# A hybrid decoder layer on one core: four layer-norm products and 24 weight low halves change engine

## The chip, the cores and the metric

The kernel runs on one NeuronCore of a Trainium2 chip. The metric is device time in microseconds (us), the median of the runs. TensorE (PE in the profile, PEld its weight loads) multiplies matrices, VectorE (DVE), ScalarE (ACT) and GpSimd (POOL) work element by element, SyncE (SP) issues most DMAs. Each engine takes its own instructions strictly in the order of its queue.

## The reference, cut to what matters

One decoder layer over 512 tokens of width 1024. RMS-normed input `h` is projected once, and three token mixers use the columns:

```python
proj = h @ w_in[i]
nq, nkv, ngate, nz, su, sv, sz, rs, rz, mg = _split_cols(proj)
y_nsa = _nsa(q, kc, vc, ks, vs, kw, vw, gate, ...)          # attention
y_sg  = _spatial_gating(su, sv, ln_g, ln_b, w_s, b_s)       # spatial gating
y_rk  = _rwkv7(rs, ...)                                     # chunked recurrence
ys = stack([y_nsa * silu(nz), y_sg * silu(sz), y_rk * silu(rz)])
...
# in _spatial_gating:
vn = ((vf - mu) * lax.rsqrt(var + LN_EPS)) * ln_g + ln_b
mixed = einsum('gts,bcsgd->bctgd', tril(w_s), vn) + b_s.T
return u * mixed
```

Then come a gated merge of the three branches, an output projection, a gated per-layer embedding and a last RMS norm.

## The kernel before, in words

**Products in two halves.** Every large product is computed with operands split into a rounded high half (type fp32r) and the rest, a low half, as three matmuls per slice of 128 rows: high x high, high x low, low x high. `wload` (L69 to L79) brings one piece of weights: SP issues a DMA into `wr` (a ring of 4 buffers, L75), ScalarE rounds it into `wh` (5 buffers, L77), and the engine that stands in `ph_["l"]` subtracts it to make `wl` (5 buffers, L78). `ph_["l"]` is a switch that the kernel sets as it goes along; `wload` reads it when it is called. A piece has at most 560 columns in all, so a block of 128 columns takes two pieces (four slices each) and a chunk of 256 or 280 columns takes four pieces (two slices each).

`fm_block` gives the product with channels on partitions: 24 matmuls of 512 columns in one PSUM tile, then an evacuation. `tm_chunk` gives it with tokens on partitions: four PSUM tiles (t = 0 to 3), 24 matmuls each, and an evacuation behind each. Both take their PSUM tile from the same two buffers (`mm_ps`), so the third tile waits until the first has been evacuated.

**The order around the change.** The recurrence runs over 8 chunks `c`, each a chain that goes from TensorE to ScalarE and VectorE and back (`r_ps`, `u_ps`, `st_ps`, copies L544 to L565; at every second chunk the norm of the output with a power on GpSimd, L587, and VectorE's L588). Projections fill TensorE meanwhile, in this order: `su`, `sv`, six merge gates `sg`, the gate `sz` of the spatial gating (L619 to L630), then `rz` and `nz` (L680 to L690). Between them stands the spatial gating itself: the layer norm of `sv`, which comes back from DRAM (L652), with statistics on VectorE (L654), the power on GpSimd (L658), and for each of 4 row tiles a subtract and multiply on VectorE (L660), the multiplication with `ln_g` on GpSimd (L661) and the addition of `ln_b` on VectorE (L662). The `sz` evacuation is a tanh on ScalarE (L624) and a product on VectorE (L625); that of `rz` and `nz` is L684 and L685.

Then the recurrence and the `sz` to `nz` buffers are closed, y1 and `rz` come back from DRAM (L713, L718), are multiplied (L719, VectorE) and split (L705 ScalarE, L706 VectorE). The attention's projections follow: values and gates in one `tm_chunk` of 280 columns (evacuation L734 to L737, ScalarE and VectorE in turn), four `fm_block`s of queries (L742 to L747), two of keys (L754 to L757). Attention and the merges come after.

The text fixes the dependencies; the order of each engine's queue is made by the tile framework's planner (`schedule_with_timeline_sim=True`), which lists the instructions by its own simulated times and gives those that stand earlier in the text precedence. `tc.issue_after` pins a few of them. In the kernel before, `ph_["l"]` is GpSimd in all of the pieces for `sz`, `rz`, `nz`, and of the attention's projections.

Of the kernel before, what the change touches and what calls it, by code (L numbers as in the profile page):

```python
# [13 lines left out]
OP = mybir.AluOpType  # L14
# [25 lines left out]
def f(ap):  # L40
    return ap.bitcast(F32)
# [3 lines left out]
def hybrid_kernel(ctx, tc, x, p, norm_g, w_in, cmp_w1, cmp_w2, cmp_pe, sg_ln_g, sg_ln_b, sg_w, sg_b,  # L45
# [3 lines left out]
    V, S, G, PE, SY = nc.vector, nc.scalar, nc.gpsimd, nc.tensor, nc.sync  # L49
# [10 lines left out]
    def mm(o, a, b, start, stop, **kw):  # L60
        return PE.matmul(o, a, b, start=start, stop=stop, **kw).ins  # L61


    ph_ = {"l": V}
# [16 lines left out]
    def wparts(segs, nk):  # L81
        per = WE // sum(s[2] for s in segs)
        hs, ls = [], []
        for k0 in range(0, nk, per):
            kn = min(per, nk - k0)
            h, l = wload([(w, c0, cn, k0) for w, c0, cn in segs], kn)
            for k in range(kn):
                hs.append(h[:, k, :])
                ls.append(l[:, k, :])
        return hs, ls  # L90
# [58 lines left out]
    def fm_block(c0, n, evac, w=None, srcH=None, srcL=None, nk=8, pool=None):  # L149
        hs, ls = wparts([(w_in if w is None else w, c0, n)], nk)  # L150
        sH, sL = (hH, hL) if srcH is None else (srcH, srcL)
        ps = pmm.tile([128, 512], F32, tag="mm", name="mm_ps")
        for k in range(nk):
            mm(ps[:n], hs[k], sH[:, k, :], k == 0, False)
            mm(ps[:n], hs[k], sL[:, k, :], False, False)
            mm(ps[:n], ls[k], sH[:, k, :], False, k == nk - 1)
        evac(ps)

    def tm_chunk(segs, srcH, srcL, nk, evac):
        n = sum(s[2] for s in segs)  # L160
        hs, ls = wparts(segs, nk)
        for t in range(4):
            ts = slice(t * 128, (t + 1) * 128)
            ps = pmm.tile([128, 512], F32, tag="mm", name="mm_ps")
            for k in range(nk):
                mm(ps[:, :n], srcH[:, k, ts], hs[k], k == 0, False)
                mm(ps[:, :n], srcH[:, k, ts], ls[k], False, False)
                mm(ps[:, :n], srcL[:, k, ts], hs[k], False, k == nk - 1)
            evac(t, ps)
# [359 lines left out]
    for c in range(8):  # L529
# [41 lines left out]
        if u == 1:  # L571
            t = c // 2
# [23 lines left out]
    for nm, off in (("su", O_SU), ("sv", O_SV)):  # L596
        for hf in range(2):
            ph_["l"] = V if (nm, hf) in LV else G
            def ev_t(t, ps, nm=nm, hf=hf):
                st = stp.tile([128, 512], F32, tag="st", name="st")  # L600
                if nm == "sz":
                    S.activation(st[:, 0:256], ps[:, 0:256], AF.Tanh, scale=0.5)
                    V.scalar_tensor_tensor(st[:, 0:256], st[:, 0:256], 1.0, ps[:, 0:256], op0=OP.add, op1=OP.mult)
                else:
                    S.copy(st[:, 0:256], ps[:, 0:256])
                SY.dma_start(dr[nm][t * 128:(t + 1) * 128, hf * 256:hf * 256 + 256], st[:, 0:256])
            tm_chunk([(w_in, off + 256 * hf, 256)], hH, hL, 8, ev_t)
    for m in range(NG):
# [5 lines left out]
        with ExitStack() as es:  # L614
            if ("sg", m) in CH:
                es.enter_context(tc.issue_after(canch[CH["sg", m]]))
            fm_block(O_MG + 1024 + m * 128, 128, ev_m)

    for nm, off in (("sz", O_SZ),):  # L619
        for hf in range(2):  # L620
            def ev_t(t, ps, nm=nm, hf=hf):
                st = stp.tile([128, 512], F32, tag="st", name="st")
                if nm == "sz":
                    S.activation(st[:, 0:256], ps[:, 0:256], AF.Tanh, scale=0.5)  # L624
                    V.scalar_tensor_tensor(st[:, 0:256], st[:, 0:256], 1.0, ps[:, 0:256], op0=OP.add, op1=OP.mult)  # L625
                else:
                    S.copy(st[:, 0:256], ps[:, 0:256])
                SY.dma_start(dr[nm][t * 128:(t + 1) * 128, hf * 256:hf * 256 + 256], st[:, 0:256])
            tm_chunk([(w_in, off + 256 * hf, 256)], hH, hL, 8, ev_t)
    sg_ctx = ExitStack()  # L630
    sp = sg_ctx.enter_context(tc.tile_pool(name="sp", bufs=2))

    z0 = sp.tile([128, 512], F32, tag="z", name="z0", bufs=1)
    lng = sp.tile([128, 512], F32, tag="lng", name="lng", bufs=1)
# [12 lines left out]
    vn = sp.tile([128, 4, 512], F32, tag="vn", name="vn", bufs=1)  # L647
# [10 lines left out]
    G.tensor_tensor(rs4, rs4, mhalf[:, 0:4], OP.pow)  # L658
    for t in range(4):
        V.tensor_scalar(vn[:, t, :], vn[:, t, :], mv[:, t, 0:1], rs4[:, t:t + 1], op0=OP.subtract, op1=OP.mult)  # L660
        G.tensor_tensor(vn[:, t, :], vn[:, t, :], lng, OP.mult)  # L661
        V.tensor_tensor(vn[:, t, :], vn[:, t, :], lnb, OP.add)  # L662
    for g in range(8):
        ps = rps.tile([128, 4, 64], F32, tag="s", name="mx_ps")
# [64 lines left out]
    vst = nsa.tile([128, 4, 2, 2, 128], R, name="vst")  # L729
    gate = nsa.tile([128, 4, 24], F32, name="gate")  # L730

    def ev_v(t, ps):
        pv = ps[:, 0:256].rearrange("p (b g d) -> p b g d", b=2, g=2)
        S.copy(vst[:, t, :, :, 0:64], pv)  # L734
        V.tensor_tensor(vst[:, t, :, :, 64:128], pv, f(vst[:, t, :, :, 0:64]), OP.subtract)
        S.activation(gate[:, t, :], ps[:, 256:280], AF.Tanh, scale=0.5)  # L736
        V.tensor_scalar(gate[:, t, :], gate[:, t, :], 0.5, 0.5, op0=OP.mult, op1=OP.add)  # L737
    tm_chunk([(w_in, O_NVS, 128), (w_in, O_NVW, 152)], hH, hL, 8, ev_v)

    for q in range(4):  # L740
# [8 lines left out]
    for b in range(2):  # L749
# [7 lines left out]
                V.tensor_tensor(K[o, g, 1, :], ps[a], f(K[a, g, 0, :]), OP.subtract)  # L757
        fm_block((O_NKS, O_NKW)[b], 128, ev_k)


    gp = ctx.enter_context(tc.tile_pool(name="gp", bufs=2))
    macc = gp.tile([128, 8, 512], F32, name="macc", bufs=1)
# [223 lines left out]
```

## Time and profile before

| | us |
|---|---|
| median of 3 runs | 767.99 (767.72, 767.99, 1015.65) |
| the profiled execution, device time | 766.05 |
| its span | 764.3 |
| TensorE busy | 729.1 (95%) |
| VectorE busy | 398.3 (52%) |
| ScalarE busy | 353.8 (46%) |
| GpSimd busy | 325.7 (43%) |

The span is the stretch from the first to the last instruction that the profiler saw; the 1.75 us to the device time lie around it. Busy shares are means over the span; what a change is worth in one stretch is read from the instructions in that stretch and from what TensorE waits for there.

### The profile page before, as it was taken

Reading aid. Unit: us, or ns where it says so; the run is one execution under the profiler, and the core shown is the slowest. Engines: PE = TensorE matmul, PEld = TensorE weight load, DVE = VectorE, ACT = ScalarE, POOL = GpSimd, SP = SyncE. Lnnn points to the kernel's source line nnn. Section 1 sums busy time; section 2 is a strip of 40 time slices with the busy share of each in tenths; the row PEclk is TensorE's granted clock in tenths of the full one; section 3 lists DMA queues with packets and bytes.
Section 4 is the critical chain, followed back from the end, with each engine's and each line's share of the span. In section 5 each row is a group of like instructions: output and inputs, shape, how many; then the busy total and the mean of one; then the engine's idle time right before and its main releaser. Section 6 shows DMA issues by size and latency. Waiting matters only on the chain.

```text
span 764.3 us, 13017 instructions
## 1 busy us (share of the span) xinstructions
PE 729.1 (95%) x4910; PEld 617.9 (81%) x4910; DVE 398.3 (52%) x748; ACT 353.8 (46%) x744; POOL 325.7 (43%) x304
## 2 busy tenths in 40 slices
PE   4899999999999899999899999989999999999996
PEld 4888877899877888778777777867877888998995
DVE  6531387758826642444649455477664222226335
ACT  6455455543362333333456564466654333226453
POOL 6444541120245443423644334534344666255563
PEclk9999999999999999999999999999999999999999
DMA  6843222125535453444533222311116433222222
GB/s 200 189 112 89 56 69 62 36 90 153 147 107 196 112 148 89 115 153 146 155 86 110 70 56 56 82 29 42 42 42 218 141 96 106 88 92 75 84 69 110
DMA packets 106688, 78.71 MB, mean 103 GB/s; under 512 B 5569, under 2 KB 97282, under 8 KB 106626
## 3 DMA queue, kind: packets, MB, share of 16 engines
q1 hardware_dynamic: 105890, 75.27, 34.5%
q10 hardware_dynamic: 736, 2.63, 0.8%
q8 instruction: 38, 0.62, 0.3%
q14 instruction: 24, 0.20, 0.1%
HBM read 67.91 MB, written 9.96 MB: 102 GB/s over the span
## 4 chain that ended last, share of the span: by engine, by line
PE 82%; DVE 7%; DMA 4%; ACT 3%; issue 2%; POOL 1%; SPq 1%; ACTq 0%; POOLq 0%; DVEq 0%
PE mm_ps L61 64%; PE s_ps L61 3%; PE o_ps L61 2%; PE g_ps L61 2%; PE p_ps L850 2%; PE Yp L61 1%; PE hid L61 1%; DMA vn<-dr_sv 1%; DMA xs__129<-in_x_dram 1%; DMA zs<-dr_nz 1%; DVE vn L662 1%; DVE mx L836 1%; ACT wh L77 1%; DVE vn L660 1%; PE mx_ps L61 1%
## 5 line engine op out<-in xcount | busy, mean ns | idle before, releaser
L78 POOL TENSOR_TENSOR wl<-wr,wh 128x512 fp32r<-128x512 f32 (+1 forms) x168 | 224.5, 1344 | 306.4 <-ACT wh L77 288.1
L77 ACT CAST wh<-wr 128x512 fp32r<-128x512 f32 (+1 forms) x194 | 119.3, 620 | 173.9 <-PE mm_ps L61 114.2
L61 PE MATMUL mm_ps<-hH,wh 128*128 128x512 f32 (+1 forms) x440 | 174.4, 396 | 6.4 <-ACT gate L736 2.7
L61 PE MATMUL mm_ps<-hH,wl 128*128 128x512 f32 (+1 forms) x440 | 172.7, 393 | 0.4 <-DVE wl L78 0.4
L61 PE MATMUL mm_ps<-hL,wh 128*128 128x512 f32 (+1 forms) x440 | 172.7, 393 | 0.0
L61 PEld LDWEIGHTS mm_ps<-hH,wh 128*128 128x128 f32 x440 | 83.6, 190 | 25.0 <-ACT gate L736 3.4
L61 PEld LDWEIGHTS mm_ps<-hH,wl 128*128 128x128 f32 x440 | 83.4, 190 | 18.6 <-DVE wl L78 0.6
L61 PEld LDWEIGHTS mm_ps<-hL,wh 128*128 128x128 f32 x440 | 83.4, 190 | 16.9 <-issue 0.4
L61 PE MATMUL mm_ps<-wh,hH 128*128 128x256 f32 (+1 forms) x224 | 64.2, 288 | 4.5 <-DVE st L625 3.3
L61 PE MATMUL mm_ps<-wh,hL 128*128 128x256 f32 (+1 forms) x224 | 64.0, 287 | 0.0
L61 PE MATMUL mm_ps<-wl,hH 128*128 128x256 f32 (+1 forms) x224 | 63.7, 285 | 0.0
L61 PEld LDWEIGHTS mm_ps<-wh,hH 128*128 128x128 f32 x224 | 42.0, 188 | 6.4 <-DVE st L625 3.5
L61 PEld LDWEIGHTS mm_ps<-wl,hH 128*128 128x128 f32 x224 | 42.1, 188 | 0.6
L61 PEld LDWEIGHTS mm_ps<-wh,hL 128*128 128x128 f32 x224 | 42.1, 188 | 0.6 <-issue 0.2
L854 DVE TENSOR_TENSOR pl<-p_ps,ph 128x512 fp32r<-128x512 f32 x40 | 27.1, 684 | 26.8 <-ACT ph L853 26.6
L61 PE MATMUL mm_ps<-ysH,wh 128*128 128x512 f32 x96 | 38.6, 402 | 0.3 <-ACT ysH L705 0.3
L61 PE MATMUL mm_ps<-ysL,wh 128*128 128x512 f32 x96 | 38.4, 400 | 0.2 <-DVE ysL L706 0.2
L61 PE MATMUL mm_ps<-ysH,wl 128*128 128x512 f32 x96 | 38.2, 398 | 0.0
L837 ACT ACTIVATE P<-s_ps,mx 128x512 f32<-128x512 f32 (+3 forms) x64 | 33.4, 531 | 7.9 <-DVE mx L836 5.5
L61 PE MATMUL mm_ps<-wh,mH 128*128 128x256 f32 x128 | 36.2, 287 | 0.6 <-DVE x L899 0.6
L61 PE MATMUL mm_ps<-wl,hT 128*128 128x256 f32 x128 | 35.8, 281 | 0.0
L61 PE MATMUL mm_ps<-wh,hT 128*128 128x256 f32 x128 | 35.8, 285 | 0.0
(336 smaller groups left out, 1450.4 us busy)
## 6 DMA issues: line engine op xcount, KB each, us to landing
wr<-in_w_in_dram SPq DMA_DIRECT2D x130, 256.0 KB
wr<-in_w_branch_dram SPq DMA_DIRECT2D x24, 256.0 KB
wr<-in_w_o_dram SPq DMA_DIRECT2D x16, 256.0 KB
wr<-in_w_ple_gate_dram SPq DMA_DIRECT2D x16, 256.0 KB
xs__129<-in_x_dram SPq DMA_DIRECT2D x4, 512.0 KB
w1t<-in_cmp_w_dram SPq DMA_DIRECT2D x4, 512.0 KB
x<-in_x_dram ACTq DMA_DIRECT2D x4, 512.0 KB
out_dram<-x SPq DMA_DIRECT2D x8, 256.0 KB
```

What stands on the lines that cost most here:

```text
L61: return PE.matmul(o, a, b, start=start, stop=stop, **kw).ins
L77: S.copy(h[:, :m], raw[:, :m])
L78: ph_["l"].tensor_tensor(l[:, :m], raw[:, :m], f(h[:, :m]), OP.subtract)
L660: V.tensor_scalar(vn[:, t, :], vn[:, t, :], mv[:, t, 0:1], rs4[:, t:t + 1], op0=OP.subtract, op1=OP.mult)
L662: V.tensor_tensor(vn[:, t, :], vn[:, t, :], lnb, OP.add)
L836: V.tensor_reduce(mx[:, hh:hh + 1], s_ps[:, :W], axis=AX.X, op=OP.max, negate=True)
L837: S.activation(P[:, hh, :W], s_ps[:, :W], AF.Exp, bias=mx[:, hh:hh + 1], accum_out=sm[:, hh:hh + 1])
L850: PE.transpose(p_ps[:, hh * 128:hh * 128 + 128], P[:, hh, kt * 128:kt * 128 + 128], ident)
L854: V.tensor_tensor(pl, p_ps, f(ph), OP.subtract)
```

## The change

Three edits. The low halves of the 8 pieces for `sz` go from GpSimd to VectorE; the multiplication with `ln_g` (4 instructions, L661) goes from GpSimd to VectorE; the low halves of the 16 pieces for the attention's projections (4 for values and gates, 8 for queries, 4 for keys) go from GpSimd to VectorE. `rz`, `nz` and everything behind the keys stay as they are. No DMA, no matmul and no buffer changes.

```diff
@@ -616,6 +616,7 @@
             fm_block(O_MG + 1024 + m * 128, 128, ev_m)
 
+    ph_["l"] = V
     for nm, off in (("sz", O_SZ),):
         for hf in range(2):
             def ev_t(t, ps, nm=nm, hf=hf):
@@ -627,6 +628,7 @@
             tm_chunk([(w_in, off + 256 * hf, 256)], hH, hL, 8, ev_t)
+    ph_["l"] = G
     sg_ctx = ExitStack()
@@ -658,7 +660,7 @@
     for t in range(4):
         V.tensor_scalar(vn[:, t, :], vn[:, t, :], mv[:, t, 0:1], rs4[:, t:t + 1], op0=OP.subtract, op1=OP.mult)
-        G.tensor_tensor(vn[:, t, :], vn[:, t, :], lng, OP.mult)
+        V.tensor_tensor(vn[:, t, :], vn[:, t, :], lng, OP.mult)
         V.tensor_tensor(vn[:, t, :], vn[:, t, :], lnb, OP.add)
@@ -728,6 +730,8 @@
     gate = nsa.tile([128, 4, 24], F32, name="gate")
+
+    ph_["l"] = V
 
     def ev_v(t, ps):
@@ -757,6 +761,7 @@
         fm_block((O_NKS, O_NKW)[b], 128, ev_k)
 
+    ph_["l"] = G
 
     gp = ctx.enter_context(tc.tile_pool(name="gp", bufs=2))
```

## Rows read from the trace of the kernel before

**Rows 1.** The page: busy us, share of the span, instructions of each engine.

```profile
PE 729.1 (95%) x4910; PEld 617.9 (81%) x4910; DVE 398.3 (52%) x748; ACT 353.8 (46%) x744; POOL 325.7 (43%) x304
```

**Rows 2.** Stretches: length, busy us of PE, PEld, DVE, ACT, POOL, clock, DMA.

```profile
225.00:254.00 29.00, 24.75 (x247) 20.98 (x247) 17.52 (x29) 6.09 (x14) 13.69 (x10) 1.00 0.59 180
254.00:350.00 96.00, 95.94 (x868) 80.74 (x867) 40.75 (x92) 33.01 (x64) 38.21 (x28) 1.00 0.41 120
350.00:372.00 22.00, 18.08 (x111) 15.84 (x110) 15.84 (x24) 10.80 (x24) 8.68 (x6) 1.00 0.56 168
372.00:402.00 30.00, 30.00 (x137) 24.14 (x136) 12.73 (x20) 14.56 (x25) 13.88 (x11) 1.00 0.41 118
```

**Rows 3.** TensorE in order of time: start, length, instruction, [idle before, releaser].

```profile
243.02 0.28 PE L61 MATMUL mm_ps<-wl,hH 128*128 128x256 f32 x1
...
250.77 0.39 PE L61 MATMUL mm_ps<-wh,hH 128*128 128x256 f32 x1 [3.34 <-DVE st L625]
...
357.88 0.40 PE L61 MATMUL mm_ps<-wh,hH 128*128 128x280 f32 x1 [1.19 <-ACT gate L736]
...
369.78 0.50 PE L61 MATMUL mm_ps<-hH,wh 128*128 128x512 f32 x1 [2.06 <-ACT gate L736]
```

**Rows 4.** VectorE in order of time, 233 to 251 and 347 to 350 us.

```profile
233.12 0.69 DVE L654 BATCH_NORM_STATS2 bs<-vn 128x6 f32<-128x512 f32 x1 [9.67 <-DMA vn<-dr_sv]
...
239.92 4.80 DVE L660 TENSOR_SCALAR vn<-vn,mv,rs 128x512 f32<-128x512 f32 x4 [0.48 <-POOL rs L658]
244.64 5.74 DVE L662 TENSOR_TENSOR vn<-vn,lnb 128x512 f32<-128x512 f32 x4
250.31 0.41 DVE L625 SCALAR_TENSOR_TENSOR st<-st,mm_ps 128x256 f32<-128x256 f32 x1
...
347.86 1.77 DVE L588 TENSOR_TENSOR yc<-yc,va 128x512 f32<-128x512 f32 x1 [3.55 <-POOL va L587]
349.54 0.68 DVE L685 SCALAR_TENSOR_TENSOR st<-st,mm_ps 128x512 f32<-128x512 f32 x1
```

**Rows 5.** Single lines: count, duration ns min/median/max, first and last start.

```profile
L660 DVE TENSOR_SCALAR vn<-vn,mv,rs x4: 534/1495/1510, 239.9 to 243.2; 128x512 f32<-128x512 f32 x4
L662 DVE TENSOR_TENSOR vn<-vn,lnb x4: 678/1756/1775, 244.6 to 249.7; 128x512 f32<-128x512 f32 x4
L588 DVE TENSOR_TENSOR yc<-yc,va x4: 691/1754/1766, 260.1 to 347.9; 128x512 f32<-128x512 f32 x4
L719 DVE SCALAR_TENSOR_TENSOR vt<-vt,par,zs x4: 739/1774/1780, 361.4 to 366.7; 128x512 f32<-128x512 f32 x4
L78 POOL TENSOR_TENSOR wl<-wr,wh x168: 1272/1302/2449, 21.1 to 747.2; 128x512 fp32r<-128x512 f32 x164, 128x560 fp32r<-128x560 f32 x4
L78 DVE TENSOR_TENSOR wl<-wr,wh x26: 675/691/1552, 16.7 to 199.0; 128x512 fp32r<-128x512 f32 x26
```

**Rows 6.** GpSimd in order of time, 241 to 248 and 344 to 368 us.

```profile
241.49 6.07 POOL L661 TENSOR_TENSOR vn<-vn,lng 128x512 f32<-128x512 f32 x4 [0.36 <-DVE vn L660]
247.53 1.71 POOL L78 TENSOR_TENSOR wl<-wr,wh 128x512 fp32r<-128x512 f32 x1
...
344.82 1.40 POOL L78 TENSOR_TENSOR wl<-wr,wh 128x560 fp32r<-128x560 f32 x1 [6.97 <-ACT wh L77]
346.18 1.64 POOL L587 TENSOR_TENSOR va<-va,mhalf 128x8 f32<-128x8 f32 x1
...
361.38 6.54 POOL L78 TENSOR_TENSOR wl<-wr,wh 128x512 fp32r<-128x512 f32 x4 [12.30 <-ACT wh L77]
```

**Rows 7.** ScalarE in order of time, 239 to 244 and 347 to 358 us.

```profile
239.58 0.62 ACT L77 CAST wh<-wr 128x512 fp32r<-128x512 f32 x1
...
243.85 0.38 ACT L624 ACTIVATE st<-mm_ps 128x256 f32<-128x256 f32 x1 [2.60 <-PE mm_ps L61]
...
347.39 0.59 ACT L684 ACTIVATE st<-mm_ps 128x512 f32<-128x512 f32 x1
...
357.12 0.63 ACT L705 ACTIVATE ysH<-zs 128x512 fp32r<-128x512 f32 x1 [3.09 <-DMA zs<-dr_y]
```

**Rows 8.** The chain that ended last, in order of time: start, length, what.

```profile
350.25 4.20 DMA dr_nz<-st
...
355.87 3.94 DMA zs<-dr_y
```

## The prediction

> **What bounds the kernel now.** I read four views in this order. The page's busy times come first: TensorE is busy for 729.1 of 764.3 us, no other engine for more than 52% [rows 1]. So an edit on VectorE or GpSimd can pay only where TensorE stands still, and the most it could ever return is the 35.2 us left. The busy times by stretch show where that is around the change [rows 2]: from 225 to 254 us TensorE idles 4.25 us, from 254 to 350 only 0.06, from 350 to 372 it idles 3.92, from 372 to 402 nothing. The change works in exactly these four stretches, so 4.25 + 3.92 = 8.2 us is the ceiling of what it can give directly.
>
> TensorE's own timeline says what those waits are [rows 3]. One of 3.34 us ends at 250.77 with VectorE's L625, the evacuation of the first `sz` tile: the third tile needs its PSUM buffer. Two of those between 350 and 372 are 1.19 us (to 357.88) and 2.06 us (to 369.78), both released by L736, the gate of the value chunk on ScalarE; the remaining 0.67 of the 3.92 are small.
>
> VectorE's and GpSimd's timelines give the cause of the first. ScalarE's tanh for that tile starts at 243.85 and takes 0.38 [rows 7]; L625 could run at 244.2, and runs at 250.31, because VectorE is filled without a gap from 239.92 by the four L660 and the four L662 [rows 4]: 10.46 us. Those eight are slow there: 1.5 and 1.76 us at the median against 0.534 and 0.678 for the quickest of the same shape [rows 5], and all the while GpSimd runs L661 and then a low half [rows 6]. A VectorE instruction beside a GpSimd one in this stretch takes some 1 us longer; the same pair of prices stands at L588 and L719 [rows 5].
>
> **The change part by part.** The switch is read when `wload` is called, so the edit moves what it names: 8 + 16 low halves and 4 products. GpSimd loses 4 x 1.5 (from L661's 6.07) + 24 x 1.30 = 37 us; VectorE gains 4 x 0.678 + 24 x 0.69 = 19.3 us [rows 5, 6]. Neither sum lies on the path as a whole. No instruction is added and no DMA is issued elsewhere.
>
> *Layer norm with the `sz` low halves.* Without GpSimd beside it, the block from 239.92 is 4 x 0.534 + 8 x 0.678 = 7.56 us. One low half falls inside it: its high half is made at 239.58 [rows 7], and GpSimd made it behind the L661 at 247.53 [rows 6]; 0.69 more, 8.25. Against 10.46 the block ends 2.2 us earlier, and so does L625. If the planner sets L625 in at 244.2, the whole 3.34 goes; if all of the contention stayed, nothing would be won: ends 0 and 3.34. I take 2.2, because the uncontended rows are of the same instructions. The other seven `sz` low halves I cost at nothing: TensorE's matmul on the fourth piece comes at 243.02 [rows 3], VectorE stands idle for 9.67 us before 233.12 [rows 4], and each takes 0.6 less than before. If that cover fails they are the slower rival below. The layer norm's result itself is not waited for until long after, so its own end counts for nothing. What is late next is nothing for a while: TensorE is full from 254 to 350, so the 2.2 us carry through as a shift.
>
> *Values and gates.* These four pieces are the wide ones. The last of them, 344.82 to 346.22 on GpSimd, is right ahead of the power L587 at 346.18, which releases L588 at 347.86 for 1.77, behind which L685 stands at 349.54 [rows 4, 6]. Without it the power can start up to 1.4 us earlier, and L588 drops to 0.69. L685 needs its tanh, ready at 347.39 + 0.59 = 347.98 [rows 7], so it gains at most 1.56; a low half or two (0.69 each) now lie on VectorE there and I take 1.3. From L685 hangs a chain that keeps its length: the store of `nz` for 4.20 us, and the load of y1 for 3.94 [rows 8], and ScalarE stands at L705 for it until 357.12 with the gate L736 queued behind [rows 7]. So the 1.19 us wait closes by 1.3.
>
> *Queries.* Before the wait that ends at 369.78 VectorE has the four L719, contended at 1.774, alone 0.739; up to 4.1 us to win, against four low halves added there (the 361.38 group [rows 6]) at 4 x 0.69 = 2.76: net 1.4 at most. L719 also needs the loads of `rz`, which come earlier by no more than the chain's 1.3, so I take half of it, 0.7. The last gate comes 1.3 + 0.7 = 2.0 us earlier, and as this is the last wait of the stretch, that is what the stretch returns, of 3.92. The other end: VectorE now stands still where a low half waits for its high half (GpSimd stood 12.30 us ahead of that group [rows 6]), and what is queued behind it are L719, L735 and L706, which ScalarE and then TensorE wait for; a piece set behind two L719 there costs 1.5 us. Ends -1.5 and 3.92.
>
> *Keys and the last queries* lie in 372 to 402, where TensorE is full and VectorE has 12.73 of 30 us taken; even all 12 pieces of queries and keys, 12 x 0.69 = 8.3 us, would hide there behind TensorE's 30. Without that cover each would cost at most its 0.69.
>
> **Sum**, against the profiled execution: 766.05 - 2.2 - 2.0 = 761.85. That execution is 1.94 below the median of 767.99, so 763.8 is what I expect of a median.
>
> **Rivals.** *(a) Given back.* L625 or the gates come earlier, but the planner, which makes its lists anew from its own times, puts other work ahead of them, or the waits come back in the attention's part. For it: VectorE's queue already lets a transfer hold up everything behind it (9.67 us at 233.12 [rows 4]). Against it: TensorE is full for 96 us behind the first gain. Price: within 1.5 us of 768.
>
> *(b) Slower: low halves stuck in VectorE's queue.* GpSimd ran its low halves beside the layer norm; VectorE runs one thing at a time. If the fourth `sz` piece is listed behind the layer norm, it comes at 239.92 + 8.25 + 0.69 = 248.9 rather than before 243.02, and TensorE stands 5.9 us in place of 3.34: 2.5 lost. With the 1.5 us of the queries it is 768.0 + 4.0 = 772. It decides from the point where the low half starts later than 242.3. For it: queues are strictly in order, and VectorE has no gap from 239.92 on. Against it: the piece's high half is ready well before, and earlier text has precedence in the lists.
>
> *(c) VectorE saturated.* In 239.92 to 250.38 VectorE is busy throughout, 10.46 of 10.46 us [rows 4]. If those durations were its own work and not contention, 4 x 0.678 + 0.69 = 3.4 us more would push L625, and TensorE with it, 3.4 us back: 771.4. The quickest L660 at 0.534 and L662 at 0.678 [rows 5] speak against it. The Trainium skill, "Perfetto Trace Analysis", section "Optimizing Scalar/DVE Operations", says that where the vector engine is saturated, handing some work to ScalarE or even GpSimd may make sense, with the reservation that GpSimd shares a read port with it. By its first half the change goes the wrong way at the one place where VectorE is full, by the second it doesn't; the trace agrees with the second half, as long as the quickest rows are the uncontended ones.
>
> *(d) Another plan altogether.* New lists may shuffle the attention's 180 us for better or worse; more than 2% either way would take 15.4 us, twice the direct ceiling. That the change does nothing is all but excluded by the text of `wload`.
>
> **Chances.** Forecast 0.54, (a) 0.20, (b) 0.15, (c) 0.06, (d) 0.05. The range: the best direct case is 768.0 - 3.34 - 3.92 = 760.7, and a kinder plan takes it some us lower, to 757; the other end takes in (a), (b) and (c), to 772.5. What a measurement of this kernel can tell from no change is about 2%, 15.4 us, so the forecast and (a) to (c) all lie within; (d) is split evenly, with a little for tails: faster 0.03, same 0.94, slower 0.03.
>
> **What would show it.** In the profile after: no GpSimd low half from 224 to 262 and from 328 to 386; L660 near 0.53 and L662 near 0.68 at the median; TensorE's wait on L625 about 1.1 us; L685 of the last `nz` tile right behind its tanh; the first wait on L736 gone and TensorE's idle time from 350 to 372 about 2 us. Wrong would be: L660 still at 1.5 us (then (c)), TensorE waiting on L78 of VectorE (then (b)), or the idle time gone here and as much of it new behind 402 us (then (a)).

## The result, and the profile after

The changed kernel takes 760.73 us (median of 760.28, 760.61, 760.85 and 762.19) against 767.99 for the kernel before: a ratio of 0.9901, 95% interval 0.9874 to 0.9928. (One execution of the kernel before took 1015.65 us and is left out; the others are 767.72, 767.99 and 768.88.) Timed once more (experiment `again`) it gave 760.97 against 767.32, 0.9911 [0.9891, 0.9931]. So it is 6.4 to 7.3 us faster: inside the range, 3 us below the forecast of 763.8, and a no-change by the 2% bound. The profiled execution of the changed kernel took 760.28 us (span 758.6), that of the kernel before 766.05: 5.8 us apart.

In the changed kernel's line numbers the layer norm is L656 (statistics), L660 (power), L662, L663 (`ln_g`) and L664 (`ln_b`); the `sz` evacuation is L626, that of `nz` L687, the gate L740, the product with `rz` L721.

The page of the changed kernel, busy times, against [rows 1]:

```profile
PE 726.5 (96%) x4910; PEld 616.3 (81%) x4910; DVE 402.8 (53%) x776; ACT 353.2 (47%) x744; POOL 286.8 (38%) x276
```

GpSimd gave up 38.9 us, and VectorE took up 4.5, not the 19.3 of the moved work. Most of the difference of 14.8 is contention that went: L660, L662, L588, L719, the four L706 behind L719 and one gate's L737 together got some 13 us quicker. The same four stretches as [rows 2], columns length, busy PE, PEld, DVE, ACT, POOL, clock, DMA:

```profile
225.00:254.00 29.00, 26.40 (x263) 22.66 (x262) 17.52 (x40) 6.30 (x14) 1.30 (x1) 1.00 0.62 190
254.00:350.00 96.00, 94.80 (x862) 79.75 (x861) 45.10 (x100) 32.56 (x65) 27.59 (x20) 1.00 0.43 121
350.00:372.00 22.00, 20.84 (x121) 18.32 (x120) 16.11 (x33) 12.09 (x26) 0.00 (x0) 1.00 0.68 197
372.00:402.00 30.00, 30.00 (x137) 23.70 (x136) 16.65 (x27) 16.71 (x32) 7.84 (x6) 1.00 0.34 96
```

Read the distance of the second number from the first: TensorE idles 2.60, 1.20 and 1.16 us, together 4.96 instead of 8.23. The 1.20 in the second stretch is new. VectorE's time from 225 to 254 is 17.52 in both kernels, with 11 instructions more after. TensorE's own timeline has each wait, as [rows 3] had:

```profile
234.82 1.02 PE L61 MATMUL st_ps<-SV,BKt 128*64 128x64 f32 x15 [1.28 <-DVE SV L549]
249.52 0.39 PE L61 MATMUL mm_ps<-wh,hH 128*128 128x256 f32 x1 [1.25 <-DVE st L626]
334.51 0.66 PE L678 MATMUL ut_ps<-ident,us 128*128 128x128 f32 x4 [0.68 <-ACT vn L679]
338.96 1.15 PE L61 MATMUL Yp<-SV,Gt 128*64 128x64 f32 x16 [0.52 <-DVE SV L549]
356.72 0.39 PE L61 MATMUL mm_ps<-wh,hH 128*128 128x280 f32 x1 [1.16 <-ACT gate L740]
```

The 3.34 us on the first `sz` evacuation are 1.25. Of the three waits on the gate (1.19, 0.68 and 2.06 before) one is left, and it is the first, hardly shorter: 1.16. VectorE's timeline over the same block as [rows 4]:

```profile
240.22 0.68 DVE L78 TENSOR_TENSOR wl<-wr,wh 128x512 fp32r<-128x512 f32 x1
241.80 1.92 DVE L662 TENSOR_SCALAR vn<-vn,mv,rs 128x512 f32<-128x512 f32 x4 [0.91 <-POOL rs L660]
243.63 1.89 DVE L663 TENSOR_TENSOR vn<-vn,lng 128x512 f32<-128x512 f32 x3
245.44 0.69 DVE L78 TENSOR_TENSOR wl<-wr,wh 128x512 fp32r<-128x512 f32 x1
246.04 0.69 DVE L663 TENSOR_TENSOR vn<-vn,lng 128x512 f32<-128x512 f32 x1
246.65 2.49 DVE L664 TENSOR_TENSOR vn<-vn,lnb 128x512 f32<-128x512 f32 x4
249.05 0.41 DVE L626 SCALAR_TENSOR_TENSOR st<-st,mm_ps 128x256 f32<-128x256 f32 x1
```

Thirteen instructions now take less time than eight did: from the first L662 to L626 it is 7.25 us, from the first L660 to L625 it was 10.39 [rows 4]. But the block starts 1.88 us later (241.80 against 239.92), so L626 comes only 1.26 earlier. TensorE gets to this wait 0.84 later than before (248.27 for 247.43: the ends of the waits, 249.52 and 250.77, less their lengths). So the wait is 2.09 shorter, but the gain at its end is 1.25. Single lines (ns min/median/max), against [rows 5]:

```profile
L662 DVE TENSOR_SCALAR vn<-vn,mv,rs x4: 541/542/545, 241.8 to 243.2; 128x512 f32<-128x512 f32 x4
L664 DVE TENSOR_TENSOR vn<-vn,lnb x4: 684/684/685, 246.6 to 248.5; 128x512 f32<-128x512 f32 x4
L588 DVE TENSOR_TENSOR yc<-yc,va x4: 693/1240/1761, 259.9 to 344.9; 128x512 f32<-128x512 f32 x4
L721 DVE SCALAR_TENSOR_TENSOR vt<-vt,par,zs x4: 748/750/753, 358.1 to 362.1; 128x512 f32<-128x512 f32 x4
```

All are within 10 ns of the quickest price of before, but for two of the four L588: 1.76 us at 259.87 and 1.75 at 321.25. Each starts beside a low half that stayed on GpSimd (259.81 and 321.18, 1.27 us each); the two quick ones (0.73 and 0.69) run beside one for at most 0.2 us. In the kernel before it was three slow ones, each beside a low half, and a quick one at 321.89 with none: a control within the kernels. Last, the chain that sets the end, from the `nz` evacuation on (start, length, what):

```profile
349.44 1.13 DVE vt L593 x4
...
350.93 0.20 ACT gate L740
...
351.92 4.01 DMA zs<-dr_y
...
355.96 0.63 ACT ysH L707
356.58 0.09 ACT gate L740
...
356.72 14.49 PE mm_ps L61 x72
```

The store of `nz` (4.20 us in [rows 8]) is not on it any more, the load of y1 still is, and behind 356.72 the chain is TensorE alone. ScalarE shows why the first wait on the gate stayed. Before (L705 is the split of y1, L736 the gate), and after (L707, L740):

```profile
357.66 0.17 ACT L736 ACTIVATE gate<-mm_ps 128x24 f32<-128x24 f32 x1
```
```profile
354.06 0.63 ACT L707 ACTIVATE ysH<-zs 128x512 fp32r<-128x512 f32 x1 [2.94 <-DMA zs<-dr_y]
...
356.49 0.17 ACT L740 ACTIVATE gate<-mm_ps 128x24 f32<-128x24 f32 x1
```

The first split starts 3.06 us earlier (354.06 for 357.12 [rows 7]), but the gate only 1.17: in the new list three splits stand ahead of it where one stood before, and the third waits until 355.96 for its part of y1. TensorE itself is 1.13 ahead there, so its wait stays as it was.

### The profile page after: what moved, and what is told of

It reads as the page before. It is cut to its first block, busy times and chain, and to the rows that moved or that the text cites. A ratio compares the mean times of both kernels' runs of the same rounds, so it can differ in the third digit from the quotient of the medians.

```text
span 758.6 us, 13009 instructions
## 1 busy us (share of the span) xinstructions
PE 726.5 (96%) x4910; PEld 616.3 (81%) x4910; DVE 402.8 (53%) x776; ACT 353.2 (47%) x744; POOL 286.8 (38%) x276
## 4 chain that ended last, share of the span: by engine, by line
PE 85%; DVE 5%; DMA 4%; ACT 2%; SPq 1%; issue 1%; POOL 0%; ACTq 0%; POOLq 0%; DVEq 0%
PE mm_ps L61 67%; PE s_ps L61 3%; PE o_ps L61 2%; PE g_ps L61 2%; PE p_ps L855 2%; DMA vn<-dr_sv 2%; PE Yp L61 1%; DMA wr<-in_w_in_dram 1%; PE hid L61 1%; DVE mx L841 1%; PE mx_ps L61 1%; DVE pl L859 1%; PE st_ps L61 1%; PE r_ps L61 1%; DVE wl L78 1%
## 5 line engine op out<-in xcount | busy, mean ns | idle before, releaser
L78 POOL TENSOR_TENSOR wl<-wr,wh 128x512 fp32r<-128x512 f32 x144 | 190.9, 1334 | 287.8 <-ACT wh L77 255.3
L78 DVE TENSOR_TENSOR wl<-wr,wh 128x512 fp32r<-128x512 f32 (+1 forms) x50 | 36.4, 729 | 19.1 <-ACT wh L77 18.8
```

The source lines that it names most:

```text
L78: ph_["l"].tensor_tensor(l[:, :m], raw[:, :m], f(h[:, :m]), OP.subtract)
```

## Experiments: the parts alone

Each experiment's kernel is timed beside the kernel before on one chip; "L626" is the wait on the first `sz` evacuation, "gates" those on L740. The theory: a GpSimd instruction with two inputs slows VectorE's in two places, and TensorE's waits there are what the change removes.

**e1_sz**: only the first edit.

```diff
+    ph_["l"] = V        # 8 sz pieces
 ...
+    ph_["l"] = G
```

> Only the 8 low halves for sz go to VectorE; the layer norm's product L661 stays on GpSimd, the attention's low halves too. Theory (VectorE is slow where GpSimd runs beside it): the four L661 are still beside the layer norm, so L660 and the addition of ln_b stay near 1.5 us each, and TensorE's wait on the first sz evacuation stays between 2.2 and 3.4 us; the time falls by 0 to 1 us against the kernel before. Rival (what counts is the order of VectorE's queue, the longer the later): two more low halves of 0.69 us in that block, the wait grows to 4 us or more, 0.7 to 1.5 us slower.

Measured: 769.73 against 768.85, 1.0011 [0.9995, 1.0028]. No gain. L626 waits 2.9 us, as expected, and L662 still lies between 542 and 1510 ns, L664 up to 1769, because the `ln_g` product stays on GpSimd. The new list brings a wait of 3.4 us on a query's copy (`qst`, L748), up to 374.78, that neither kernel of the study has.

**e2_ln**: only the `ln_g` products.

```diff
-        G.tensor_tensor(vn[:, t, :], vn[:, t, :], lng, OP.mult)
+        V.tensor_tensor(vn[:, t, :], vn[:, t, :], lng, OP.mult)
```

> Only the four products with ln_g go to VectorE; every low half stays on GpSimd. Theory: GpSimd has only two low halves left beside the layer norm, so most of L660, the product and the addition take 0.53 to 0.69 us, the block shrinks from 10.5 to 8 to 9 us and TensorE's wait of 3.34 us to 1 to 2: 1.3 to 2.3 us faster than before. Rival (VectorE is saturated there by work of its own): four products more on it make the block longer than 10.5 us and the wait longer than 3.34, 0 to 3 us slower.

Measured: 764.61 against 768.85, 0.9943 [0.9924, 0.9962], 4.2 us where 1.3 to 2.3 were expected, about twice what the wait can give: L626 waits 1.5 instead of 3.3, and the gates keep their 3.5 us. L664 is at 676 to 680 ns; L662 still reaches 1500, beside two low halves that GpSimd makes from 238.74 to 241.43. So the layer norm's gain belongs to the product's move, and the waits alone do not account for it.

**e3_att**: only the third edit, 16 pieces.

```diff
+    ph_["l"] = V        # ahead of the value and gate chunk
 ...
+    ph_["l"] = G        # behind the keys
```

> Only the 16 low halves of the attention's projections go to VectorE. Theory: TensorE's three waits on the gate of the value chunk, 3.9 us together, shrink to about 1.2 as in the changed kernel, the four L719 go from 1.5 to 0.75 us, and the time falls by 2.5 to 3.5 us. The wait on the first sz evacuation stays at 3.3. Rival (the two edits help each other only through the plan as a whole): less than 1 us, or waits of TensorE on low halves of VectorE.

Measured: 764.12, 0.994 [0.9921, 0.996], 4.7 us, again more than expected. L626 waits 3.3 as before; of the gates the first wait is left, 1.6.

**e4_sz_ln**: the first two edits.

> The sz low halves and the products with ln_g go to VectorE, the attention's low halves stay on GpSimd: the change without its third edit. Theory: L660 at 0.5, the wait on the first sz evacuation 1.2 us, and the three waits on the value chunk's gate back at 3 to 4 us; 1 to 2.5 us faster than before. With e3_att the parts add up to the whole change within 1 us. Rival: the parts do not add up, because each plan is another one.

Measured: 763.88, 0.9931 [0.9913, 0.995], 5.0 us. L626 1.1, gates 3.3 in three waits, the 1.2 on SV as in the whole. e3 and e4 together make 9.7 us, the whole change 6.4 to 7.3. By these medians the parts do not add up to the whole within 1 us, which was expected of them, and each recovers more alone than the idle time it removes. But each part's interval reaches 1.5 us either way and that of the whole 2, so the runs do not settle by how much.

**e_v** and **e_qk** split the third edit: the 4 wide pieces of values and gates, or the 12 of queries and keys.

```diff
     tm_chunk([... values and gates ...])
+    ph_["l"] = G        # e_v; in e_qk G before the chunk and V here
```

> Of the 24 low halves only the four wide ones of the values and gates go to VectorE; layer norm, sz, queries and keys as before. Theory: the power L587 starts up to 1.4 us earlier, L588 takes 0.69 instead of 1.77, and the nz store starts about 1.3 us earlier; the first two of TensorE's three waits on the value chunk's gate close, the third (2.1 us) stays, because the four L719 still run beside GpSimd's low halves of the queries: 1.3 to 2 us faster than before. Rival (the queries' low halves do it all): within 0.7 us of the kernel before, all three waits as they were.

> Of the 24 low halves only the twelve of the queries and keys go to VectorE; layer norm, sz, values and gates as before. Theory (the four L719 and the last gate of the value chunk are held up by GpSimd's work beside them, and a wait of TensorE of some 2 us is followed, in most executions, by a stretch at 1.2 GHz): the third and longest wait on the gate, 2.1 us, shrinks below 1, the L719 go to 0.75 us, no low stretch between 355 and 378, and the time is 2.5 to 4.5 us under the kernel before. Rival (the wide pieces and the nz store before them open the path, these twelve are hidden): within 1 us of the kernel before.

Measured: e_v 766.73, 0.9983 [0.9967, 0.9999]; e_qk 765.27, 0.9961 [0.9941, 0.9981]: 0.6 and 2.2 us, both less than their theories had, 2.8 together against 4.7 for both at once (within the intervals). In e_v the gates still cost 2.8 us, 0.8 in the first wait and 2.0 in the last, and the product with `rz` (L721) lies at 740 to 1792 ns, since GpSimd still makes query pieces there. In e_qk L721 is at 742 to 753, and the last wait is gone, as expected; but the first has grown to 2.1, and a low stretch of the clock (0.92 from 357 to 378) is there although none was expected. The forecast's order was wrong: values and gates were given 1.3 of 2.0 us, and the larger share is the queries'.

## Experiments: is it contention, and what else

**e_beside** puts GpSimd work back beside the layer norm without giving it anything of the computation's: four `tensor_scalar` whose result nobody reads.

```diff
+    gj = sp.tile([128, 512], F32, tag="gj", name="gj", bufs=1)
+    for t in range(4):
+        G.tensor_scalar(gj, lng, rs4[:, t:t + 1], None, op0=OP.mult)
```

> The changed kernel with four GpSimd multiplications of a 128x512 tile added beside the layer norm: they start when the power L660 is done, read ln_g, write a tile that nobody reads, and nobody waits for them. Theory (VectorE is slow because GpSimd works beside it): the subtract and the two vector products go from 0.5 to 0.7 back to 1.2 to 1.8 us for as long as the four run, the wait on the first sz evacuation grows from 1.2 to between 3 and 6 us, and the time is 1.5 to 5 us above the changed kernel. Rival (the gain is that GpSimd's queue and the hand-over between the engines are off the path): the added work hurts nobody, within 0.7 us of the changed kernel.

Measured: 764.39 against 767.32, 0.9962 [0.9947, 0.9977]; `again`, on the same chip, is 760.97, so 3.4 us lost. VectorE, and under it GpSimd, in this kernel's line numbers:

```profile
242.16 2.50 DVE L665 TENSOR_SCALAR vn<-vn,mv,rs 128x512 f32<-128x512 f32 x4 [0.91 <-POOL rs L660]
...
248.41 2.90 DVE L667 TENSOR_TENSOR vn<-vn,lnb 128x512 f32<-128x512 f32 x4
251.24 0.41 DVE L626 SCALAR_TENSOR_TENSOR st<-st,mm_ps 128x256 f32<-128x256 f32 x1
```
```profile
242.23 8.81 POOL L663 TENSOR_SCALAR gj<-lng,rs 128x512 f32<-128x512 f32 x4
```

The same VectorE instructions take 9.08 us to L626 instead of 7.25, with nothing in VectorE's queue changed; L626 holds TensorE for 3.1 us instead of 1.1. So GpSimd's activity alone brings the wait back: contention is shown. The 1.2 to 1.8 us that were expected of each instruction did not come: the size depends on the GpSimd operation. Beside this one-input form the median `tensor_scalar` takes 686 ns and the median addition 679 (at most 1091), not the 1495 and 1756 of [rows 5], and each GpSimd instruction takes 2.13 us. Of the eight two-input products and additions, all beside GpSimd, three took 1.09 us and five their quickest price. The wait is 1.9 us of the 3.4; this profile also has two low stretches of the clock that `again` lacks (0.86 from 246 to 258, 0.92 from 357 to 378). The Trainium skill, "SBUF — State Buffer", section "Who interferes with whom", says that VectorE and GpSimd share a pair of ports as an exclusive lock, and that a VectorE instruction with two SBUF inputs contends with a GpSimd one that reads SBUF. Contention agrees; that such a pair always costs, or costs a whole instruction of the other, does not: an L667 at 1.09 beside a GpSimd instruction of 2.13 lost 0.41, and five of the eight lost nothing.

**again** and **before2** run the two kernels once more.

> The changed kernel once more, on the same chip as the next three and as a second profile. Theory (the gain is TensorE's shorter waits, 4 to 5 us, and, on top, fewer stretches at the lower clock, which in the profiles so far began behind a wait or a thin stretch of TensorE): 7 to 8.5 us faster than before, runs within 2.5 us of each other where those of the kernel before lie 6 us apart; a profile with at most one low stretch between 100 and 700 us. Rival (the waits alone): 4 to 6 us faster, runs as far apart as before.

> The kernel before once more, for a second profile. Theory (waits of TensorE of 2 us and more are followed by a low stretch of the clock in most executions, and the first profile was one without): the same waits, 3.3 us at 250 and 3.9 in three near 360 to 370, and at least one low stretch right behind one of them; its device time then lies 1 to 4 us above the 766.05 of the first profile. Rival (the low stretches come from elsewhere): none near 250 or 370 again.

`again`: 760.97 us, 6.4 below the kernel before, between its theory and its rival; waits SV 1.8, L626 1.1, gate 1.0. `before2`, one execution: 770.90, span 769.2, 4.85 us longer than the first profile, with the same waits from 225 to 372 (L625 3.3, SV 0.9, gates 3.7). In two places there only the granted clock differs. Three stretches of `before2`, and the same of the first profile of before and of the changed kernel (the last column but two is the clock):

```profile
246.00:258.00 12.00, 8.68 (x88) 7.98 (x87) 8.01 (x17) 2.79 (x6) 2.50 (x3) 0.86 0.18 50
357.00:378.00 21.00, 17.32 (x78) 14.06 (x78) 16.35 (x19) 11.31 (x24) 10.94 (x8) 0.92 0.60 181
555.00:576.00 21.00, 19.47 (x97) 15.79 (x96) 13.00 (x35) 10.39 (x31) 8.79 (x8) 0.92 0.18 46
```
```profile
246.00:258.00 12.00, 8.66 (x109) 8.00 (x110) 8.96 (x18) 3.09 (x7) 4.01 (x3) 1.00 0.20 57
357.00:378.00 21.00, 17.38 (x84) 14.26 (x85) 17.12 (x20) 12.30 (x25) 12.14 (x8) 1.00 0.60 176
555.00:576.00 21.00, 19.47 (x98) 15.61 (x98) 11.96 (x29) 11.04 (x31) 8.91 (x9) 0.92 0.22 58
```
```profile
246.00:258.00 12.00, 10.75 (x129) 10.04 (x127) 9.95 (x24) 4.09 (x9) 0.17 (x1) 1.00 0.29 81
357.00:378.00 21.00, 21.00 (x104) 17.61 (x104) 16.18 (x29) 12.22 (x25) 0.00 (x0) 1.00 0.64 185
555.00:576.00 21.00, 19.47 (x102) 15.63 (x101) 13.15 (x28) 11.10 (x32) 10.37 (x9) 1.00 0.30 83
```

As an estimate, 0.86 over 12 us is 1.7 us lost (12 x 0.14), 0.92 over 21 us another 1.7. The times agree roughly: `before2` ends the wait on L625 1.15 us ahead of the first profile (249.62), is 0.36 behind it at the last tanh of `nz` and 1.71 at the first exponential of the attention, so the two stretches cost 1.5 and, on gates that waited 0.25 less, 1.6. The rest of the 4.85 is lost between 547 and 581 (1.4, with 0.92 in both profiles, open) and behind 588, where a wait of 1.7 instead of 0.3 on L705 is followed by a third low stretch (0.86 from 588 to 600). TensorE's timeline of `before2` right behind the last wait on the gate:

```profile
369.92 0.79 PE L61 MATMUL mm_ps<-hH,wh 128*128 128x512 f32 x1 [2.03 <-ACT gate L736]
370.51 0.63 PE L61 MATMUL mm_ps<-hL,wh 128*128 128x512 f32 x1
370.94 0.63 PE L61 MATMUL mm_ps<-hH,wl 128*128 128x512 f32 x1
...
373.42 0.39 PE L61 MATMUL mm_ps<-hH,wl 128*128 128x512 f32 x1
373.64 0.40 PE L61 MATMUL mm_ps<-hH,wh 128*128 128x512 f32 x1
```

Matmuls start 0.43 us apart (370.51 to 370.94), and from 373.42 on 0.22: the 1.2 and the 2.4 GHz level. The first profile of before, the only one the forecast had, shows no such stretch at either place, only the one at 555 to 576.

**e_pin** and **e_pin2** keep the changed kernel's edits and pin VectorE's order, since the waits that are left stand behind instructions that wait for a transfer: the statistics L656 at 233.56 (5.54 us idle for `dr_sv`) hold the recurrence's SV copy L549.

```diff
-        V.bn_stats(bs, vn[:, t, :])
+        with tc.issue_after(svc[0]):       # e_pin2: svc[0] if t < 2 else snc[0]
+            V.bn_stats(bs, vn[:, t, :])
 ...
+        with tc.issue_after(stv[0]), tc.issue_after(svc[1]):
+            V.tensor_tensor(vn[:, t, :], vn[:, t, :], lnb, OP.add)
```

`svc`, `snc` and `stv` are the copies L549 and L564 of each chunk and the `sz` evacuations.

> The changed kernel with three places in VectorE's queue pinned: the layer norm's statistics come behind the first chunk's state copy L549, and the additions of ln_b come behind the first sz evacuation and behind the second chunk's L549. Theory (what is left of TensorE's waits between 225 and 254 us, 1.3 and 1.2, is only the order of VectorE's queue): both waits fall below 0.5 us and the time falls by 1.5 to 2.5 us against the changed kernel, more if a low stretch of the clock goes with them. Rival (the waits come back further on, since nothing but TensorE's own list is late there): within 0.7 us of the changed kernel.

Measured: 759.69, 0.9895 [0.987, 0.9919], 1.3 us below `again`, just short of its theory and less than its own interval's width. The waits on SV and L626 are gone, but 1.9 us on the statistics' chain replace them: the recurrence's L559 and L564 of the same chunk are queued behind the last statistics, whose transfer came later than in the changed kernel (241.12 for 238.88).

> The kernel with pins, with the third and fourth statistics of the layer norm also set behind the first chunk's last copy L564, on which TensorE waited 1.9 us in the version before. Theory (a transfer that comes late holds up whatever stands behind it in VectorE's queue): TensorE's waits between 225 and 254 fall below 0.7 us together, 1 to 2 us faster than with the first pins, 8 to 10 faster than before. Rival (the wait moves on to the next thing again): within 0.7 us of the first pins, 7 to 8 faster than before.

Measured: 756.10 against 767.49, 0.985 [0.9826, 0.9875], 11.4 us below the kernel before (8 to 10 were expected) and 4.9 below `again`, of which 2.9 are that kernel's waits on SV and L626; its profile also has 1.00 from 555 to 576, that of `again` 0.92 (1.7). Its stretches and VectorE's timeline:

```profile
225.00:254.00 29.00, 29.00 (x315) 25.68 (x314) 20.67 (x46) 8.88 (x18) 2.44 (x2) 1.00 0.59 194
254.00:350.00 96.00, 95.48 (x847) 81.13 (x845) 45.94 (x97) 31.93 (x63) 27.21 (x20) 1.00 0.45 129
```
```profile
227.32 0.42 DVE L549 COPY SV<-u_ps 64x256 f32<-64x256 f32 x1 [0.51 <-PE u_ps L61]
231.48 0.69 DVE L657 BATCH_NORM_STATS2 bs<-vn 128x6 f32<-128x512 f32 x1 [3.74 <-DMA vn<-dr_sv]
...
243.69 0.41 DVE L626 SCALAR_TENSOR_TENSOR st<-st,mm_ps 128x256 f32<-128x256 f32 x1
244.02 0.41 DVE L549 COPY SV<-u_ps 64x256 f32<-64x256 f32 x1
244.35 2.48 DVE L666 TENSOR_TENSOR vn<-vn,lnb 128x512 f32<-128x512 f32 x4
```

TensorE is busy for the whole 29 us. The evacuation and the copy come ahead of the `ln_b` additions, which nobody is waiting for.

**e_best** adds to this a move of the return of y1 and `rz` behind the value chunk (the moved lines are left out here), with the split of y1 pinned behind the second gate, so that this gate no longer stands behind it:

```diff
+        with tc.issue_after(gt_[1]):
+            split(y1H[:, q, :], y1L[:, q, :], zs, 0.5)
```

> That, and the return of y1 and rz moved in the text behind the chunk of values and gates, with the split of y1 set behind the second gate on ScalarE and VectorE's share following it. Theory: the last wait on the gate L736 (1.1 us) goes, since ScalarE no longer stands at the split for a transfer with a gate behind it; 0.5 to 1.5 us faster than e_pin2. Rival (the later tiles' gates now stand behind the same split): the wait is as long or longer, and the time within 0.7 us of e_pin2 or above it.

Measured: 755.98 against 767.49, 0.9838 [0.9815, 0.9861]. The wait on the gate is gone (TensorE busy for 22.00 of 22 us from 350), but the time is e_pin2's to 0.1 us. This miss is open: its profile has 0.92 at 555 to 576 where e_pin2's has 1.00, 1.7 us, which would cover the 1.4 that the gate cost there, but that stretch is low or not from one execution to the next (1.00 in the first profile of the changed kernel, 0.92 in `again`). e_pin2 and e_best both beat the two kernels of the study.

## Why the prediction was right in kind and 3 us short

*The bound and the mechanism* held. TensorE's idle time in the two places was what could be returned; the instructions fell to their quickest prices (0.542 for 0.534, 0.684 for 0.678), the low halves left GpSimd (two that the edits don't touch, at 259.81 and 383.21, lie inside the bounds that the forecast had set too wide), and e_beside brings the wait back with GpSimd alone.

*Layer norm with `sz`, -2.2.* The wait on L626 is 1.25, near the forecast of about 1.1, but by luck: L626 came 1.26 earlier instead of 2.2, and TensorE reached it 0.84 later. The block gained more than foreseen, 3.14 us (7.25 for 10.39) where 2.2 was worked out: consecutive instructions overlap in the records by some 0.07 us, and four L662 of 542 ns take 1.92. But that the 2.2 us "carry through as a shift" failed: the start of the block moved by 1.88, since the last statistics come at 238.88 instead of 237.68 behind the transfer of `dr_sv` (1.20), L559 and L564 now stand between them and L659 (0.32), and the power L660 on GpSimd comes later behind L659 and takes 1.30 us instead of 1.01 (0.36). Two new waits, 0.68 and 0.52, followed at 334 and 339, and that on SV went from 0.8 to 1.28. At the last tanh of `nz` (346.37, was 347.39) 1.0 us of the 2.2 is there. The steps that failed are that the block would start when it did, and "what is late next is nothing for a while".

*Values and gates, -1.3, and queries, -0.7.* TensorE idles 1.16 of 22 us instead of 3.92: 2.76 rather than 2.0. The sum is near, its two terms are not. L687 comes right behind its tanh, 1.53 closer than L685 stood (1.3 was worked out), and the `nz` store left the chain. But "the 1.19 us wait closes by 1.3" failed: it is 1.16, since two more splits of y1 stand ahead of the gate. All 2.74 us of the other two waits went, where 0.7 was given to the queries and the 0.68 was passed over as small. Ahead of the last gate VectorE's L735 came 4.38 earlier (L739 at 364.61 for 368.99): the first product with `rz` starts 3.33 earlier (358.11 for 361.44), since its load is issued 3.06 earlier (355.44 for 358.50) and not 1.3, and the queue from it to L735 is 1.05 shorter, with a gate's contended `tensor_scalar` of 1.27 that had not been costed. The first exponential of the attention came 4.4 us earlier; 3.27 of it is idle time of 225 to 372 (8.23 less 4.96), and 1.1 lies in rows where TensorE counts as busy. That part stays open.

*The clock* was not in the sum. Of the 5.8 us between the profiles, 1.0 was there at 347, 3.4 came by the first exponential, and 1.7 between 545 and 578, where the clock was 0.92 before and 1.00 after; 0.3 was lost again behind it. The medians are 7.3 apart because that of the kernel before lies 1.94 above its profile and that of the changed kernel 0.45. The forecast added the 1.94 without asking what it was, and so took it to be the same for both kernels. That it is one more low stretch in a median execution of the kernel before, as `before2` has at 250 and 370, fits its size but is not shown. The executions scattered less too: 765.76 to 770.35 in 21 of the kernel before, 760.29 to 761.72 in 6 of the changed one, on one chip.

*The rivals.* (a) is seen in small (the two new waits, 1.2 us, and the first wait on the gate, held by the new list of ScalarE). (b) and (c) did not come: TensorE nowhere waits on L78 of VectorE in these stretches, and the block with four more products on VectorE is shorter. The new lists of (d) cost e1_sz its wait of 3.4 us and may be why e3 and e4 exceed the whole: this was not settled.

## What to carry to other kernels

Where an engine looks full, first compare one line's quickest and median durations of the same shape: if they stand 1 to 2.6, as 0.68 to 1.76 here, taking the other engine's work over can make it shorter. A shorter wait is not yet a gain: compare when it ends, since the engine that waits may have come later. A wait of TensorE costs more than its length where the clock drops behind it (some 1.5 us here), so price one wait with both levels, and take more than one profile of the kernel before when the clock is at stake. What remained here was not work but order: pinning what somebody waits for ahead of what waits for a transfer gave 4.9 us more, beside 6.4 to 7.3 for the change itself.

## What the runs showed of the hardware that was not expected

*The clock behind a wait.* By the granted clock of the 14 profiles: of seven with a wait of 2.9 us or more on the `sz` evacuation, six show a low stretch at 246 to 258 (0.72 or 0.86); of seven with 1.5 or less, none. At 357 to 378, of eight with 1.8 us or more of waits in all, seven are low (0.92, or 0.96); of six with 1.6 or less, none. The two exceptions are both the first profile of the kernel before, so in these profiles the drop goes with the wait in most cases, not in all. A wait is not needed for one either: before, the changed kernel, e3_att, e_beside and e_pin have a low stretch (0.80 to 0.93) from 70 to 90, where TensorE is busy for 20.00 of 20 us. e_v shows both (waits 3.3 and 2.8), e3_att one of each; the clock is the last column but two:

```profile
246.00:258.00 12.00, 8.69 (x95) 7.93 (x96) 7.91 (x17) 2.98 (x7) 2.65 (x3) 0.86 0.20 57
357.00:378.00 21.00, 18.43 (x83) 15.12 (x84) 14.95 (x18) 11.11 (x23) 11.61 (x8) 0.92 0.56 163
```
```profile
246.00:258.00 12.00, 8.67 (x70) 8.12 (x70) 8.29 (x16) 2.15 (x5) 2.87 (x2) 0.72 0.17 46
357.00:378.00 21.00, 19.44 (x101) 16.45 (x100) 16.74 (x31) 13.14 (x27) 0.00 (x0) 1.00 0.71 199
```

The waits were not varied alone, so this is a coincidence in 14 profiles, not a proof of cause. The Trainium skill, "Perfetto Trace Analysis", section "Matmul Optimizations", says that the matmul engine scales its power with its use and should be fed back to back; the rows at the two waits agree, with a price, estimated at 1.7 us for each stretch at 0.86 over 12 or 0.92 over 21 us; the stretch from 70 to 90 does not.

*One-input GpSimd work beside VectorE* is not free, but much cheaper than two-input work: beside a GpSimd `tensor_scalar` of 128x512 (2.13 us; no run has it alone) the median VectorE `tensor_scalar` took 0.14 us more and the two-input instructions 0.41 or nothing; with two inputs on both sides VectorE's price was 1.76 for 0.68.
